# A list schedule with other durations and margins, and one copy moved from ScalarE to GpSimd

## The chip, the core and the metric

The kernel runs on one core of a Trainium2 chip. The metric is the device time of one execution in microseconds (us): the median of several runs. The profiler's engine names are used throughout: PE is TensorE's matmuls and PEld its weight loads, DVE is VectorE, ACT is ScalarE, POOL is GpSimd, and SPq is the queue of SyncE, from which this kernel issues all of its transfers. Each engine works through its own queue in order.

## The reference, cut to what matters

Two transformer blocks over 256 tokens of width 2048, in float32. The first block mixes sparse attention (NSA, 8 heads of 128) and an RWKV7 recurrence (16 heads of 64); the second has a layer A (differential attention) and a layer B (gated linear attention). Most of the work are products of the 2048-wide activations with weight matrices. The change sits in the recurrence:

```python
def rwkv7_mixer(feat, mu, w0, w2, a0, a2, k_k, k_a, r_k, ln_w, ln_b):
    ...
    aa = -kk
    bb = kk * a4
    def step(state, inp):
        r_t, w_t, k_t, v_t, a_t, b_t = inp
        sa = jnp.einsum('bhij,bhj->bhi', state, a_t)
        state = (state * w_t[:, :, None, :] + sa[..., None] * b_t[:, :, None, :]
                 + v_t[..., None] * k_t[:, :, None, :])
        return state, jnp.einsum('bhij,bhj->bhi', state, r_t)
    xs = tuple(z.transpose(1, 0, 2, 3) for z in (r4, w4, k4, v4, aa, bb))
    _, y = lax.scan(step, state0, xs)
```

The kernel doesn't step through 256 tokens. It takes them in 4 chunks of 64, and inside a chunk it solves a triangular system, for which a unit lower triangular matrix is inverted, in diagonal blocks of 32 by 32.

## The kernel before

**The weight stream.** Every weight matrix is cut into column groups (rk0, v0, kvc, rk2, v2, v3, q1, ...) and row tiles of 128. A `load` puts a raw tile `wr` into one of 4 buffers (512 KB a transfer, on SP's queue). ACT rounds it into the high part `wh` (fp32r), DVE subtracts to get the low part `wl`, 3 buffers each; then PE does three products per 128 columns (`wh` with `xh`, `wh` with `xl`, `wl` with `xh`) into `acc`. A tile of 128x1024 feeds 24 matmuls of 256 columns.

**The recurrence.** `rwkv_group(g, ...)` handles 4 of the 16 heads and is called for g = 0 to 3. Per group: decays `P`, the norm factor `ni` (a power on POOL), its square `sq` for the norm matmul `pnb`; small POOL copies `PC`; the four score matrices `AB` (matmuls `pA`); gathering of their diagonal blocks through DRAM (`db`, 4 transfers, then `blocks<-db`) so that 32 blocks of 32x32 lie on 32 partitions of the tile `blocks` (half `Y`); and the inversion by 30 steps of two POOL TENSOR_TENSORs each (`bt<-blocks`, `blocks<-blocks,bt`), a chain of 60 instructions, each depending on the one before. Then a transposed copy of `Y` into the other half `X`. `Y` and `X` go to DRAM (`dy`, `dx`), come back as `M1` (4 transfers; the trace calls them M) and `X` (2 transfers), and are used by the matmuls `pT` (on X), `pY`, `pX` and `pU`, after which the group's states follow chunk by chunk.

**Beside it** stand the compression products of NSA: `w1_00` to `w1_13` (weights, 8 loads of 512 KB, w_10 and so on in the rows) against windows, matmuls `ph`, then ACT's copy `hs`, matmuls `pz`, a tanh by ACT `ht`.

**What sets the order.** No order is written out by hand. Every call is recorded in a `Plan`; `flush` (L272, the line that all profile rows show) issues them in the order that `schedule` finds. It is a list schedule: it keeps a modelled time for each engine, lets each engine take the ready operation of the best priority, and appends it to the order. `Op.model` gives an operation's modelled duration, `LATENCY` what passes between two engines, `MARGIN` an addition for whatever TensorE waits for, `POOL_MARGIN` one for POOL's results that another engine waits for, `DMA_ISSUE` and its neighbours a transfer. Since the queues run in order, a modelled time that is too short puts an instruction ahead of work that could have gone first. The inversion chain is recorded with `nc.priority(1)`.

## Time and profile before

| what | before |
|---|---|
| median of 3 runs | 1500.48 us (1498.72 to 1500.61) |
| the profiled execution | 1499.45 us |
| its span, first to last instruction | 1497.7 us |
| PE busy | 1465.4 us (98%) |
| PEld, DVE, ACT, POOL busy | 89%, 63%, 51%, 20% |
| mean granted TensorE clock | 0.992 |

The profiled execution takes 1.75 us more than its span. Busy time is the union of an engine's instructions; matmuls are pipelined, so a row's duration (0.28 us for 256 columns at full clock) is longer than the distance to the next one (0.12 us). The granted clock is 1.00 at 2.4 GHz and 0.50 at 1.2 GHz. In rows, `[5.85 <-ACT hs]` says that the engine stood idle for 5.85 us before the instruction and that ACT's `hs` ended the wait.

### The profile page before, as it was taken

How to read it: one execution, taken by the hardware profiler on the slowest of the kernel's cores; microseconds unless marked ns; L12 is line 12 of the kernel's file. 1: busy time of each engine (PE TensorE's matmuls, PEld its weight loads, DVE VectorE, ACT ScalarE, POOL GpSimd, SP SyncE). 2: the span in 40 equal slices, each digit the busy share in tenths (PEclk: the TensorE clock that was granted, in tenths of full speed). 3: DMA queues.
4: the chain of work that ended last, by engine and by line, in shares of the span. 5: the costliest groups of instructions: out<-in, count | busy, mean ns of one | idle time of the engine just before them, and what ended most of it. 6: DMA issues, size and time to landing. Idle time of an engine off the chain costs nothing.

```text
span 1497.7 us, 25998 instructions
## 1 busy us (share of the span) xinstructions
PE 1465.4 (98%) x10205; PEld 1326.1 (89%) x10205; DVE 944.1 (63%) x1630; ACT 769.4 (51%) x1257; POOL 296.4 (20%) x398
## 2 busy tenths in 40 slices
PE   8999899999999999999999999999999999999999
PEld 8988789889989988778888888889999998988999
DVE  5775565375756765766666666756665459665554
ACT  6542354354454544757575757655443355455432
POOL 0139833812900000030404040100010001000000
PEclk9999999999999999999999999999999999999999
DMA  9546524444434467665555556555665554555563
GB/s 338 186 125 204 155 79 126 148 139 147 155 98 132 151 209 231 201 207 181 174 178 172 180 170 229 169 185 196 207 201 182 172 175 146 174 211 185 181 211 127
DMA packets 91963, 263.52 MB, mean 176 GB/s; under 512 B 19960, under 2 KB 26512, under 8 KB 91840
## 3 DMA queue, kind: packets, MB, share of 16 engines
q1 hardware_dynamic: 91840, 261.86, 54.5%
q8 instruction: 80, 1.31, 0.3%
q14 instruction: 43, 0.35, 0.1%
HBM read 253.92 MB, written 7.90 MB: 175 GB/s over the span
## 4 chain that ended last, share of the span: by engine, by line
PE 78%; POOL 3%; DVE 2%; DMA 1%; issue 1%; ACT 1%; SPq 0%; ACTq 0%; DVEq 0%; POOLq 0%
PE acc_Bo L272 6%; PE acc_Ao L272 6%; PE acc_o L272 6%; PE acc_Ag L272 6%; PE acc_Av L272 6%; PE acc_Aq L272 6%; PE acc_Bg L272 6%; PE acc_Ak L272 5%; PE acc_Bv L272 5%; PE acc_Bq L272 3%; PE acc_Bk L272 3%; PE acc_q L272 3%; PE acc_zb L272 3%; PE acc_za L272 2%; POOL bt L272 2%; POOL blocks L272 1%
## 5 line engine op out<-in xcount | busy, mean ns | idle before, releaser
L272 POOL TENSOR_TENSOR blocks<-blocks,bt 32x30 f32<-32x30 f32 (+14 forms) x120 | 84.3, 702 | 9.4
L272 POOL TENSOR_TENSOR bt<-blocks 32x30 f32<-32x30 f32 (+14 forms) x120 | 77.9, 649 | 9.2
L272 PE MATMUL acc_rk<-xh,wh_rk 128*128 128x256 f32 x256 | 74.1, 291 | 1.1 <-ACT wh_rk L272 0.9
L272 PE MATMUL acc_rk<-xh,wl_rk 128*128 128x256 f32 x256 | 73.8, 289 | 0.5 <-DVE wl_rk L272 0.5
L272 PE MATMUL acc_rk<-xl,wh_rk 128*128 128x256 f32 x256 | 73.1, 286 | 0.2 <-DVE xl L272 0.2
L272 PE MATMUL acc_Ao<-mAh,wl_Ao 128*128 128x256 f32 x256 | 72.7, 284 | 0.0
L272 PE MATMUL acc_Bo<-mBh,wl_Bo 128*128 128x256 f32 x256 | 72.6, 284 | 0.0
L272 PE MATMUL acc_Ao<-mAh,wh_Ao 128*128 128x256 f32 x256 | 72.5, 283 | 0.0
L272 PE MATMUL acc_Ao<-mAl,wh_Ao 128*128 128x256 f32 x256 | 72.4, 283 | 0.0
L272 PE MATMUL acc_Bo<-mBl,wh_Bo 128*128 128x256 f32 x256 | 72.4, 283 | 0.0
L272 PE MATMUL acc_Bo<-mBh,wh_Bo 128*128 128x256 f32 x256 | 72.3, 283 | 0.0
L272 DVE TENSOR_TENSOR wl_Bo<-wr_Bo,wh_Bo 128x1024 fp32r<-128x1024 f32 x32 | 39.2, 1225 | 45.0 <-ACT wh_Bo L272 45.0
L272 DVE TENSOR_TENSOR wl_rk<-wr_rk,wh_rk 128x1024 fp32r<-128x1024 f32 (+1 forms) x33 | 41.2, 1250 | 39.9 <-ACT wh_rk L272 36.7
L272 DVE TENSOR_TENSOR wl_Ao<-wr_Ao,wh_Ao 128x1024 fp32r<-128x1024 f32 x32 | 41.2, 1292 | 36.3 <-ACT wh_Ao L272 36.3
L272 DVE TENSOR_TENSOR wl_o<-wr_o,wh_o 128x1024 fp32r<-128x1024 f32 x32 | 39.2, 1225 | 37.2 <-ACT wh_o L272 37.2
L272 ACT ACTIVATE wh_Bo<-wr_Bo 128x1024 fp32r<-128x1024 f32 x32 | 33.9, 1058 | 53.1 <-PE acc_Bo L272 49.8
L272 DVE TENSOR_TENSOR wl_Bg<-wr_Bg,wh_Bg 128x1024 fp32r<-128x1024 f32 x32 | 39.2, 1224 | 34.8 <-ACT wh_Bg L272 34.8
L272 ACT ACTIVATE wh_rk<-wr_rk 128x1024 fp32r<-128x1024 f32 (+1 forms) x33 | 34.1, 1033 | 45.6 <-PE acc_rk L272 22.9
L272 DVE TENSOR_TENSOR wl_Bv<-wr_Bv,wh_Bv 128x824 fp32r<-128x824 f32 (+1 forms) x40 | 40.5, 1017 | 26.6 <-ACT wh_Bv L272 26.3
L272 ACT ACTIVATE wh_Ao<-wr_Ao 128x1024 fp32r<-128x1024 f32 x32 | 33.8, 1057 | 45.5 <-PE acc_Ao L272 38.7
L272 PE MATMUL acc_Bv<-wl_Bv,xBh 128*128 128x412 f32 (+1 forms) x160 | 56.4, 353 | 0.8 <-DVE wl_Bv L272 0.8
L272 DVE TENSOR_TENSOR wl_Ag<-wr_Ag,wh_Ag 128x1024 fp32r<-128x1024 f32 x32 | 39.2, 1224 | 28.0 <-ACT wh_Ag L272 28.0
(769 smaller groups left out, 5429.5 us busy)
## 6 DMA issues: line engine op xcount, KB each, us to landing
wr_o<-w SPq DMA_DIRECT2D x32, 512.0 KB, 4.0
wr_Aq<-w SPq DMA_DIRECT2D x32, 512.0 KB, 3.8
wr_Ak<-w SPq DMA_DIRECT2D x32, 512.0 KB, 3.5
wr_Av<-w SPq DMA_DIRECT2D x32, 512.0 KB, 4.3
wr_Ag<-w SPq DMA_DIRECT2D x32, 512.0 KB, 3.5
wr_Ao<-w SPq DMA_DIRECT2D x32, 512.0 KB, 3.5
wr_Bg<-w SPq DMA_DIRECT2D x32, 512.0 KB, 3.3
wr_Bo<-w SPq DMA_DIRECT2D x32, 512.0 KB, 4.2
```

The lines of the kernel that those rows point to most:

```text
L272: op.issued = getattr(getattr(self.nc, op.eng), op.method)(*op.args, **op.kw)
```

## The change

Three things change. `Op.model` gets other durations for TensorE (a matmul's cost no longer depends on its column position, and each matmul is given its `part`: the size and the position of the piece of the array that it uses) and for POOL's 32-partition TENSOR_TENSORs (200 + 2.9 ns an element where 150 + 1.65 or 2.1 stood). The planner's margins grow (`MARGIN` 200 to 700 ns, `POOL_MARGIN` 500 to 1500 ns), an issued transfer takes 340 ns of SP's modelled time instead of 60, a change of part size costs PE 170 ns, and a matmul at another column position than its predecessor counts half. And the transposed copy of the inverted blocks goes from ACT to POOL. No other operation is added or removed; all others may move in their queues.

```diff
@@ -110,15 +110,19 @@
         if self.dma:
             return n * out.shape[0] / 90
         if self.eng == "tensor":
-            at = out.start_partition() // 32
             if self.method == "transpose":
+                self.part = (4, 4, 0, 0)
                 return 109 if out.shape[-1] > 64 else 53
             cols, m = size(self.args[2]), size(self.args[1])
+            quarters = lambda n: 1 if n <= 32 else 2 if n <= 64 else 4
+            k = self.args[1].shape[0]
+            self.part = (quarters(k), quarters(m), self.args[1].start_partition() // 32 if k <= 64 else 0, out.start_partition() // 32 if m <= 64 else 0)
             if self.args[1].dtype == F32R:
-                return max(107, cols / 2.4)
+                return max(110, 13 + cols / 2.4)
             if m > 64:
-                return max(218, 4 + cols / 0.6)
-            return 3 + cols / 0.6 if at == 0 else 26.5 * -(-m // 32)
+                return max(220, 6 + cols / 0.6)
+            return 6 + cols / 0.6
         src = [x for x, write in self.uses if not write]
         psum = any(x.space == bass.MemoryType.PSUM for x in src)
         column = lambda x: isinstance(x, bass.AP) and size(x) == 1
@@ -138,8 +142,7 @@
         if self.kw.get("op") == OP.pow:
             return 300 + 165 * n
         if self.method == "tensor_tensor":
-            spread = all(any(not s for s, _ in x.ap[1:]) for x in src)
-            return 150 + (1.65 if spread else 2.1) * n
+            return 200 + 2.9 * n if out.shape[0] == 32 else 150 + 2.1 * n
         return 127 + 3.4 * n
 
 
@@ -157,9 +160,10 @@
         "gpsimd": {"tensor": 310, "vector": 60, "scalar": 180, "gpsimd": 102, "sync": 200},
     }
 
-    MARGIN, DMA_MARGIN, POOL_MARGIN = 200, (400, 1500), 500
+    MARGIN, DMA_MARGIN, POOL_MARGIN = 700, (400, 1500), 1500
     TABLE = 1283
-    DMA_ISSUE, DMA_START, DMA_EACH, DMA_END = 60, 950, 450, 990
+    SWITCH = 170
+    DMA_ISSUE, DMA_START, DMA_EACH, DMA_END = 340, 950, 450, 990
 
     def __init__(self, nc):
         self.nc = nc
@@ -169,6 +173,7 @@
         self.prio, self.chain, self.after = 0, None, ()
         self.free = dict.fromkeys(self.ENGINES, 0.0)
         self.log_table = False
+        self.part = None
         self.dma_queue = self.dma_engine = 0.0
         self.buffers, self.alive = {}, set()
         for eng in self.ENGINES:
@@ -382,7 +387,15 @@
             if eng == "scalar" and op.args[2] in (AF.Exp, AF.Tanh, AF.Ln) and self.log_table != (op.args[2] == AF.Ln):
                 self.log_table = not self.log_table
                 at += self.TABLE
-            op.start, op.end = at, at + op.cost
+            cost = op.cost
+            if eng == "tensor":
+                old, self.part = self.part, op.part
+                if old and old[:2] != op.part[:2]:
+                    at += self.SWITCH
+                elif old and old[3] != op.part[3]:
+                    cost /= 2
+            op.start, op.end = at, at + cost
             self.free[eng] = op.end
             op.seen = op.end + 200
 
@@ -882,7 +895,7 @@
                 tmp = self.sb(f"bt{g}_{k}", [128, 256], "bt", bufs=2)[gp, 0:k * n].rearrange("p (i j) -> p i j", j=n)
                 G.tensor_tensor(tmp, Y[:, 0:k, k:k + 1].to_broadcast([32, k, n]), Y[:, k:k + 1, k + 1:32].to_broadcast([32, k, n]), op=OP.mult)
                 G.tensor_tensor(Y[:, 0:k, k + 1:32], Y[:, 0:k, k + 1:32], tmp, op=OP.add)
-        S.activation(X.rearrange("p i j -> p j i"), Y, AF.Copy)
+        G.tensor_copy(X.rearrange("p i j -> p j i"), Y)
         dy = self.dram.tile([4, 4, 2, 32, 32], F32, name=f"dy{g}")
         nc.sync.dma_start(dy.rearrange("q h c s t -> (q h c) s t"), Y)
         dx = self.dram.tile([4, 4, 2, 32, 32], F32, name=f"dx{g}")
```

ACT's queue around the copy of group 0. Before, the copy stands between two `wh` of the rk2 weights and ahead of `hs`:

```order
L272 ACTIVATE wh_rk_10_470<-wr_rk_10_469 128x1024
L272 ACTIVATE wh_rk_12_474<-wr_rk_12_473 128x1024
L272 ACTIVATE blocks<-blocks 32x32x32
L272 ACTIVATE wh_rk_14_478<-wr_rk_14_477 128x1024
L272 ACTIVATE hs_458<-ph_443 128x128
L272 ACTIVATE ht_462<-hz_461 128x30
L272 ACTIVATE wh_v_0_495<-wr_v_0_494 128x1024
```

ACT's queue at the same place after:

```order
L277 ACTIVATE wh_rk_10_470<-wr_rk_10_469 128x1024
L277 ACTIVATE wh_rk_12_474<-wr_rk_12_473 128x1024
L277 ACTIVATE hs_458<-ph_443 128x128
L277 ACTIVATE ht_462<-hz_461 128x30
L277 ACTIVATE wh_rk_14_478<-wr_rk_14_477 128x1024
L277 ACTIVATE kc<-pkc 128x2x15
L277 ACTIVATE wh_v_0_495<-wr_v_0_494 128x1024
```

The copy is gone from ACT, and `hs` and `ht` stand ahead of the last `wh` of rk2. No copy of `blocks` is left in ACT's queue for any of the four groups.

SP's queue at the same place, before: the group's inverse goes out with dy and dx, and comes back as M and X. `w_10` to `w_13` are weights for the `ph` matmuls.

```order
L272 DMA wr_v_4_497<-w 128x1024
L272 DMA w_10_468<-cw 128x1024
L272 DMA dy_230<-blocks 32x1024
L272 DMA wr_v_8_500<-w 128x1024
L272 DMA dx_231<-blocks 32x1024
L272 DMA cw_481<-cw 128x128
L272 DMA w_11_472<-cw 128x1024
L272 DMA w_12_476<-cw 128x1024
L272 DMA wr_v_12_503<-w 128x1024
L272 DMA M_240<-dy_230 32x8x32 x4
L272 DMA w_13_480<-cw 128x1024
L272 DMA X_241<-dx_231 32x8x32 x2
```

SP's queue at the same place after:

```order
L277 DMA wr_v_0_494<-w 128x1024
L277 DMA dy_230<-blocks 32x1024
L277 DMA w_10_468<-cw 128x1024
L277 DMA wr_v_4_497<-w 128x1024
L277 DMA M_240<-dy_230 32x8x32 x3
L277 DMA dx_231<-blocks 32x1024
L277 DMA M_240<-dy_230 32x8x32
L277 DMA w_11_472<-cw 128x1024
L277 DMA w_12_476<-cw 128x1024
L277 DMA cw_481<-cw 128x128
L277 DMA wr_v_8_500<-w 128x1024
L277 DMA X_241<-dx_231 32x8x32 x2
```

dy stands ahead of `w_10` and of `wr_v_4` where it stood behind both. The load that starts group 0's inversion (blocks<-db_199) stands behind `wr_kvc_415` (the third load of kvc), where it stood behind `wr_kvc_427` (the seventh).

POOL's queue where group 0's inversion starts, before: `PC` and `ni` belong to the next group (1).

```order
L272 MEMSET p02p 128x2
L272 MEMSET M_240 32x8x32 x2
L272 MEMSET p12p 128x2
L272 COPY PC_326<-P_314 64x2 x6
L272 TENSOR_TENSOR ni_320<-n_319,mhalf 128x8
L272 MEMSET blocks 32x32
L272 TENSOR_TENSOR bt_30_200<-blocks 32x30
L272 TENSOR_TENSOR blocks<-blocks,bt_30_200 32x30
L272 TENSOR_TENSOR bt_29_201<-blocks 32x58
```

POOL's queue after, the start of the inversion and a piece further on:

```order
L277 MEMSET p02p 128x2
L277 MEMSET blocks 32x32
L277 TENSOR_TENSOR bt_30_200<-blocks 32x30
L277 TENSOR_TENSOR blocks<-blocks,bt_30_200 32x30
L277 TENSOR_TENSOR bt_29_201<-blocks 32x58
...
L277 COPY PC_326<-P_314 64x2
L277 TENSOR_TENSOR bt_22_208<-blocks 32x198
L277 COPY PC_326<-P_314 64x2
L277 TENSOR_TENSOR blocks<-blocks,bt_22_208 32x22x9
L277 TENSOR_TENSOR ni_320<-n_319,mhalf 128x8
L277 TENSOR_TENSOR bt_21_209<-blocks 32x210
```

The inversion stands ahead of group 1's `PC` copies and `ni`, which are now spread between its steps. POOL's copy of `blocks` stands behind the last step of its own group and the first step of the next. On PE, 1182 matmuls stood ahead of the first `pT` of group 0, and 1115 do now (of those gone, 58 are 256-column products of the weight stream and 9 are `ph`); ahead of the first `ph` of `w_10` stand 25 products of the weight stream fewer.

## Rows read from the trace of the kernel before

**Rows 1.** The page: busy time, share of the span and instructions of each engine
```profile
PE 1465.4 (98%) x10205; PEld 1326.1 (89%) x10205; DVE 944.1 (63%) x1630; ACT 769.4 (51%) x1257; POOL 296.4 (20%) x398
```
**Rows 2.** Stretches: PE, PEld, DVE, ACT, POOL busy (instructions); PEclk; DMA share; GB/s
```profile
105.00:112.00 7.00, 4.39 (x21) 3.35 (x20) 3.46 (x6) 1.06 (x1) 6.17 (x16) 0.76 0.45 156
...
149.00:160.00 11.00, 5.15 (x42) 4.84 (x40) 2.17 (x5) 4.41 (x6) 8.52 (x23) 0.69 0.58 178
...
295.00:307.00 12.00, 6.00 (x32) 5.51 (x32) 5.67 (x11) 4.89 (x5) 2.75 (x10) 0.72 0.50 132
...
416.00:426.00 10.00, 7.16 (x36) 6.49 (x35) 6.57 (x16) 4.92 (x14) 0.00 (x0) 0.66 0.66 185
```
**Rows 3.** Stretches, PE alone: length, PE busy, PEclk, DMA share, GB/s; their sum
```profile
155.69:159.40 3.71, 3.71 (x18) 0.50 0.96 329
...
sum 17.98, PE 16.49; mean PE 4.12
```
**Rows 4.** Timeline at 149 to 156 us, PE and then ACT: start, duration, instruction, [idle before]
```profile
149.44 0.28 PE L272 MATMUL acc_rk<-xh,wh_rk 128*128 128x256 f32 x1
149.56 0.28 PE L272 MATMUL acc_rk<-xl,wh_rk 128*128 128x256 f32 x1
155.69 0.64 PE L272 MATMUL pz<-cst,hs 128*128 128x32 f32 x2 [5.85 <-ACT hs L272]
...
152.71 1.93 ACT L272 ACTIVATE blocks<-blocks 32x1024 f32<-32x1024 f32 x1 [7.96 <-POOL blocks L272]
...
155.39 0.24 ACT L272 ACTIVATE hs<-ph 128x128 f32<-128x128 f32 x1
```
**Rows 5.** Timeline at 298 us, ACT
```profile
298.30 1.93 ACT L272 ACTIVATE blocks<-blocks 32x1024 f32<-32x1024 f32 x1 [10.13 <-POOL blocks L272]
```
**Rows 6.** Timeline at 413 to 419 us, ACT and then SP's queue
```profile
413.45 2.08 ACT L272 ACTIVATE blocks<-blocks 32x1024 f32<-32x1024 f32 x1 [5.75 <-POOL blocks L272]
...
418.95 0.35 SPq L272 DMA_DIRECT2D wr_q<-w  x1
```
**Rows 7.** Timeline at 100 to 111 us, POOL and then DVE
```profile
100.67 5.78 POOL L272 COPY PC<-P 64x2 f32<-64x2 f32 x6 [1.97 <-ACT P L272]
...
109.77 1.19 POOL L272 TENSOR_TENSOR bt<-blocks 32x84 f32<-32x84 f32 x1
...
108.21 0.50 DVE L272 TENSOR_SCALAR sq<-ni 128x512 f32<-128x512 f32 x1 [2.92 <-POOL ni L272]
...
109.45 1.32 DVE L272 TENSOR_TENSOR wl_kvc<-wr_kvc,wh_kvc 128x1024 fp32r<-128x1024 f32 x1
```
**Rows 8.** The waits by pair: us in total, times, longest
```profile
ACT blocks L272 <- POOL blocks L272: 23.8, 3, 10.1
```
**Rows 9.** The tile blocks: duration ns min/median/max, first and last start, forms
```profile
L272 POOL TENSOR_TENSOR bt<-blocks x120: 225/560/1677, 108.2 to 412.9; 32x30 f32<-32x30 f32 x8, 32x58 f32<-32x58 f32 x8, 32x84 f32<-32x84 f32 x8, 32x108 f32<-32x108 f32 x8
...
L272 ACT ACTIVATE blocks<-blocks x4: 1927/2004/2116, 152.7 to 413.5; 32x1024 f32<-32x1024 f32 x4
```
**Rows 10.** GpSimd's copies: the tile PC, and the timeline at 1250 us
```profile
L272 POOL COPY PC<-P x24: 178/284/4661, 66.8 to 330.4; 64x2 f32<-64x2 f32 x24
...
1250.82 3.82 POOL L272 COPY k<-kd 128x128 f32<-128x128 f32 x1 [135.78 <-DVE kd L272]
```
**Rows 11.** Timeline, SP's queue and then PE; DMA landing of the tile dx
```profile
98.06 0.31 SPq L272 DMA_DIRECT2D blocks<-db  x1
...
152.70 0.34 SPq L272 DMA_DIRECT2D dy<-blocks  x1
...
160.67 0.92 SPq L272 DMA_DIRECT2D X<-dx  x2
...
159.57 0.64 PE L272 MATMUL ph<-w,win 128*32 128x128 f32 x16
...
169.62 0.56 PE L272 MATMUL pT<-X,AB 32*32 32x32 f32 x23
...
DMA to landing us min/median/max: 2.0/3.0/5.8
```

## Prediction

> **What bounds the kernel now.** The page's busy times come first: PE is busy for 1465.4 of the 1497.7 us of the span [rows 1]. So PE is the bound, and a change of order can win only two things: the 32.3 us in which PE stands idle, and time in which its clock is low. The next view is the table of stretches, which shows where these are. Four short places hold most of it [rows 2]: idle there is 7.00 − 4.39 = 2.61, 11.00 − 5.15 = 5.85, 12.00 − 6.00 = 6.00 and 10.00 − 7.16 = 2.84 us, together 17.30. The other 15.0 us lie scattered over some 1460 us. In the same four stretches, and in no other of the table, the granted clock is well under 1. Looked at closely, each idle piece is followed by matmuls at a clock of 0.50, that is 1.2 GHz; the four pieces hold 16.49 us of PE work [rows 3]. What that costs: in the piece shown 18 instructions take 3.71 us; at the 0.12 us between two 256-column products at full clock [rows 4] they would take 2.16, so 42% are lost, or 6.9 us over the four; if all of them took exactly twice as long it would be 8.25. I take 7.
>
> Then the timelines say who is late at each place. At 149.56 us PE stops for 5.85 us until ACT's `hs`. ACT had not been busy: it stood idle for 7.96 us in front of its copy of `blocks`, which waits for the last step of GpSimd's inversion at 152.7 us, and `hs`, at 155.39, was queued behind it [rows 4]. At 298.30 it is the same with `wh_v`: ACT waits 10.13 us for the inversion, with the weights' rounding behind the copy [rows 5]. At 413.45 ACT waits 5.75 us and, after its 2.08 us copy, has a heap of softmax work and two `wh_q` to catch up on; besides, a load of `wr_q` is issued only at 418.95 [rows 6], since `dy`, `dx` and the M transfers ahead of it in SP's queue waited for the same inversion. Summed by pair, ACT's waits for the inversion are 23.8 us in three pieces [rows 8]: three of four groups. The fourth place, the stretch from 105 us, is another thing: PE waits for `pnb`, that for DVE's `sq`, which starts at 108.21 after 2.92 us of idling, since POOL needed 5.78 us for six copies of 64x2 and then made `ni` [rows 7].
>
> **The change, part by part.**
>
> *The copy leaves ACT.* Nothing of ACT's queue waits for the inversion any more. At places 2 and 3 ACT then has its `hs` and `wh_v` done when their inputs are there, some 5.85 and 6.00 us earlier than PE needed to stop for. At place 4 the copy's wait and its 2.08 us go too. Gain: the idle time of these places, 14.7 us.
>
> *The new durations of POOL's steps.* Group 0's inversion takes 152.70 − 108.2 = 44.5 us [rows 9, 11]. The old order, with ACT's copy too early at three groups, shows that it was planned as shorter. Now its `blocks` load stands four weight loads earlier in SP's queue, and one such load feeds 24 products of 0.12 us, so 2.88 us of PE: issue at 98.06 − 11.5 = 86.5 us [rows 11].
>
> *`ni` and `PC` of group 1* now stand between steps of group 0's inversion, `ni` after 18 of 60. They no longer keep `sq` waiting if the norm is at hand; the six copies are not in front of `ni` in a block, since only two are. Gain at place 1: 2.61 us, perhaps 2.
>
> *The clock* returns with the idle time: 7 us of the sum, 6.9 to 8.25 by the above.
>
> So far −17.3 − 7 = −24.3.
>
> *POOL's copy, 4 times.* The trace has no such copy on POOL. From below: ACT's took 1.93 to 2.12 us [rows 9]. From nearby: POOL's steps have a median of 0.56 us [rows 9] at a mean of 165 elements (30, 58, 84 and so on, 4960 over 30 steps), 3.4 ns an element, which gives 3.5 us for 1024; they read two operands and the copy one. From far: `k<-kd` took 3.82 us for 128 elements a partition at a time when DVE was busy without a gap [rows 10], which would give 8 x 3.82 = 30.6 us. I take 2.5 us, by the steps, which run on the same partitions and at the same hour. Cover: `X` is needed only by `dx`, and ahead of `dx` in SP's queue stand the `dy` transfer and three M transfers that wait for it. The next group's inversion is behind the copy on POOL and 2.5 us later for it, in a chain of 45 to 50; its cover is counted in the next term. On the path: 0.
>
> *A new wait: the inverse comes back late.* On PE the first `pT` stands 58 products and 9 `ph` earlier, 58 x 0.12 + 9 x 0.04 = 7.3 us. It ran at 169.62 [rows 11]; less the lost time of places 1 and 2 (2.61 + 5.85 idle, and 42% of two low-clock pieces of 4.12 us, their mean [rows 3], 3.5; together 12.0), less 7.3, PE is there at 150.3 us. The inverse: `blocks` issued at 86.5, landed after 3.0 (2.0 to 5.8, by the transfers of `dx` [rows 11]), 44.5 us of steps, and between them `ni` (108.2 − 106.45 = 1.7) and six `PC` (6 x 0.284 at their median [rows 10], 5.78 as at 100.67 [rows 7]): it ends at 89.5 + 44.5 + 3.4 to 7.5 = 137.4 to 141.5 us. From the end of the steps to the issue of the last X transfer it took 160.67 + 0.92 − 152.70 = 8.9 us, with about as many transfers between, and 3.0 to land: X is there at 149.3 to 153.4, with slow landings at 159. So PE waits for 0 to 3.1 us, at the outside 8. `w_10` now stands behind `dy` on SP: issued within 1 us of the inversion's end and landed 3 later, at 141.4 to 145.5; its `ph` ran at 159.57, less 12.0, less 25 x 0.12, so it is wanted at 144.6. That fits by medians and no more. Behind `dy` stand `w_10`, `wr_v_4` and everything after, but of raw weight tiles there are four. I take +2 (0 to +8, the clock's fall included) for groups 0 and 1 together.
>
> *Order on the array.* In PE's order 355 neighbouring pairs of small matmuls of one part size now lie at different positions, where 273 did; changes of size are 175 instead of 176. 23 alternating `pT` pass in 0.56 us, 16 `ph` at one position in 0.64 [rows 11], 0.024 against 0.040 each: 82 x 0.016 = 1.3. I take −1 (0 to −1.3).
>
> *The wider margin for PE's operands* can only touch the 15.0 us elsewhere: −1 (from −4 to +3; the places are many and each is tiny).
>
> Sum: −24.3 + 2 − 1 − 1 = −24.3. The profiled execution took 1499.45 us, which gives 1475.2; it lies 1.0 below the median of the runs, so on that scale 1476.
>
> **A rule that speaks against it.** In the trace, POOL's step of 84 elements at 109.77 took 1.19 us and ended at 110.96, just after DVE's `wl` subtract from 109.45 to 110.77 [rows 7]; and the first of the six copies that took 5.78 us began while DVE ran without a gap [rows 7], where the median copy takes 0.284 [rows 10]. The Trainium skill ("SBUF — State Buffer", "Who interferes with whom") says that a DVE instruction with two inputs in SBUF and a GpSimd instruction that reads SBUF shut each other out, for as long as the first of the two runs. By that rule the copy can start late by one subtract or several, and the trace agrees with it in the 1.19 us step. The same section would have the next `wl` subtract wait for the end of the copy, which no row here shows; at 2.5 us, with three `wl` buffers of 2.88 us of PE work each, it would stay hidden.
>
> **The rivals.**
>
> (a) *The inverse is late at groups 0 and 1.* Both have no slack to speak of. For it: `w_10` and X fit to within 2 us by medians, and landings go up to 5.8. Against: four raw tiles and the margin. Price: the outer case of 8 us once, some 2 to 4 at group 1: about 9 more than forecast, 1485.
>
> (b) *The change doesn't do what it says: the wait goes from ACT to SP's queue.* `dy` stands as early as before or earlier, and the loads behind it are held until the inversion ends. For it: place 4 has it already, with `wr_q` at 418.95 [rows 6]. Against: at 149 and 298 us PE waited for ACT and not for a raw tile. Price: place 4 loses 2.84 us of idling [rows 2] and 42% of a low-clock piece of 4.12 [rows 3], 4.6 us; kept there and new at two more, 13.7 us: 1490. Were SP's waits to cost at each place what ACT's do now, only place 1's 2.61 us would be won: 1498, no change that can be told.
>
> (c) *Slower: POOL's copy is starved by DVE.* A copy that runs as `k<-kd` did takes 30.6 us [rows 10]. At groups 0 and 1 nearly all of the excess of 28 us goes to PE's wait for X: 1476 + 2 x 28 = 1532. It decides from the point where a copy takes 2.5 + (24 + 3) / 2 = 16 us. The rule of the Trainium skill above would allow it, where DVE's two-input work is dense. Against it: steps of the inversion ran all the time beside such work with a median of 0.56 us and at most 1.677 [rows 9].
>
> **How the numbers follow.** Chances: the forecast 0.64, (a) 0.17, (b) 0.13, (c) 0.06. What a measurement of this kernel can tell from no change is 0.2%, 3 us. Faster by more: 0.64 + 0.17 and 0.09 of (b), 0.90; within it 0.04, (b) at its full price; slower 0.06. The range: the forecast's own goes from −17.3 − 8.25 − 4 − 1.3 = −30.9 (1469) to −17.3 − 6.9 + 3 + 8 = −13.2 (1487). To leave out no more than 2 in 10 it reaches over (a) to the edge of (b): 1468 to 1490.
>
> **What would show it.** In the profile after: no copy of `blocks` on ACT and no wait of ACT for POOL's `blocks`; four POOL copies of 2 to 3.5 us; PE busy at about 1457 (1465.4 less 7 and 1) and idle at 15 to 18 us; in the stretches 105, 149, 298 and 416, clock 1.00. (a) would show as a wait of PE for the transfer of X or of `w` at about 140 to 155 us with clock 0.50 behind it; (b) as waits of ACT for `wr` transfers while SP stands at `dy`; (c) as a POOL copy of over 15 us. The forecast is wrong if PE's idle time stays above 25 us, or if its busy time doesn't fall.

## The result, and the profile after

The changed kernel takes 1491.28 us (median of 5 runs, 1488.82 to 1492.53); the kernel before took 1500.61 beside it (1498.72 to 1501.98). The ratio is 0.9938, 95% interval 0.9925 to 0.9951. It is faster, but by 9.3 us and not by 24, and the time lies 1.3 us above the forecast's range of 1468 to 1490. The profiled execution took 1491.25 us, its span is 1489.4, that is 8.3 less than before.

The page's busy times of the changed kernel, to be held against [rows 1]:

```profile
PE 1462.6 (98%) x10205; PEld 1322.8 (89%) x10205; DVE 952.9 (64%) x1630; ACT 762.0 (51%) x1253; POOL 313.3 (21%) x402
```

PE is busy for 2.8 us less and idle for 26.8 us where it was 32.3. The forecast had 8 less and some 16, and named idle time above 25 us as a sign of being wrong. DVE is busy for 8.8 us more, with as many instructions.

The most useful cut is between the two blocks, at the first transpose of the second block (`tp`). The stretches of the kernel before:

```profile
0.00:614.10 614.10, 589.69 (x4901) 0.98 0.52 165
614.10:1497.70 883.60, 875.75 (x5304) 1.00 0.57 184
```

And of the changed kernel (length, PE busy, PEclk, DMA share, GB/s):

```profile
0.00:597.10 597.10, 582.42 (x4901) 0.99 0.53 169
597.10:1489.40 892.30, 880.17 (x5304) 0.99 0.57 182
```

The first block, with the four places, is 17.0 us shorter: 9.7 us less of idling (24.4 to 14.7) and 7.3 us less of PE time. The second block, of which the forecast said only that the wider margins might touch it, is 8.7 us longer: 12.1 us of idling instead of 7.9, and 4.4 us more of PE time for the same 5304 products.

**What went as forecast.** ACT has no copy of `blocks` and no wait for GpSimd's `blocks`; the waits of 5.85, 6.00 and 2.84 us at places 2 to 4 [rows 2] are not there. GpSimd's copies, in the rows of the tile:

```profile
L277 POOL COPY blocks<-blocks x4: 2048/2114/2132, 145.2 to 396.4; 32x1024 f32<-32x1024 f32 x4
```

2.1 us each, where 2.5 were taken. The inverse of group 0 was done early, and PE still had to wait for it, as the term of the new wait said. The timeline, SP's queue and then PE:

```profile
144.85 0.34 SPq L277 DMA_DIRECT2D dy<-blocks  x1
...
152.42 1.16 SPq L277 DMA_DIRECT2D X<-dx  x2
...
154.80 0.64 PE L277 MATMUL ph<-w,win 128*32 128x128 f32 x16 [1.43 <-DMA w<-cw]
158.18 0.87 PE L277 MATMUL pT<-X,AB 32*32 32x32 f32 x32 [1.59 <-DMA X<-dx]
```

`dy` left 7.9 us earlier than in [rows 11], the first `pT` came 11.4 us earlier, and on the way there PE waited 1.43 us for a `w` and 1.59 for X, 3.0 in all (forecast: 2).

**Place 1 stayed.** The same wait for `sq` as in [rows 7], timeline of POOL, DVE and PE:

```profile
104.95 1.69 POOL L277 TENSOR_TENSOR ni<-n,mhalf 128x8 f32<-128x8 f32 x1
...
106.98 1.07 DVE L277 SCALAR_TENSOR_TENSOR k<-fr,par,k 128x256 f32<-128x256 f32 x2
107.98 1.61 DVE L277 TENSOR_TENSOR wl_kvc<-wr_kvc,wh_kvc 128x1024 fp32r<-128x1024 f32 x1
109.51 0.41 DVE L277 TENSOR_SCALAR sq<-ni 128x512 f32<-128x512 f32 x1
...
109.98 1.11 PE L277 MATMUL pnb<-cst,sq 128*128 128x128 f32 x4 [2.79 <-DVE sq L277]
```

`ni` ends at 106.64, 1.5 us earlier than before. But DVE, which had stood idle for it before, is now late itself: `sq` stands behind two `k` and a `wl` of 1.61 us (1.22 for the `wl` at 105.06 us). All this runs beside GpSimd's inversion, which started behind 108 us before and starts at 90.8 us now.

**The moved copy cost something at group 1.** DVE, ACT and PE when GpSimd's copy runs (194.25 to 196.36 us):

```profile
194.59 2.53 DVE L277 COPY AV<-fv 128x256 f32<-128x256 f32 x2
...
198.81 0.72 ACT L277 ACTIVATE P<-L 128x256 f32<-128x256 f32 x2 [1.83 <-DVE L L277]
199.44 0.49 ACT L277 ACTIVATE sq<-fk,par 128x256 f32<-128x256 f32 x1
...
199.98 0.83 PE L277 MATMUL pn<-cst,sq 128*128 128x2 f32 x6 [1.15 <-ACT sq L277]
```

The first of the two DVE copies lasted 2.13 us and ended 0.36 us after GpSimd's copy did; the tile's row has it as the longest of eight, and in the kernel before none took more than 0.29:

```profile
L277 DVE COPY AV<-fv x8: 284/386/2134, 53.6 to 307.5; 128x256 f32<-128x256 f32 x8
```

From it hang `L`, ACT's `P` and `sq` behind it, and PE's `pn`: 1.15 us of idling and then, from 201.75 us on, a granted clock of 0.50 for 16 products.

**The second block.** POOL and PE in layer B, timeline:

```profile
1235.91 3.55 POOL L277 COPY k<-kd 128x128 f32<-128x128 f32 x1 [136.49 <-DVE kd L277]
...
1239.52 0.80 PE L277 MATMUL pB<-q,k 128*128 128x128 f32 x2 [2.94 <-POOL k L277]
```

And PE's stretch behind the wait:

```profile
1239.52:1246.00 6.48, 6.48 (x37) 0.50 0.11 44
```

This copy took 3.82 us before [rows 10], hardly different. What differs is PE's queue: before, 7 products of `acc_Bv` stood between the `pB` part that needs `kd` and the one that needs `k`, and the wait was 1.49 us:

```profile
1254.69 0.49 PE L272 MATMUL pB<-q,k 128*128 128x128 f32 x2 [1.49 <-POOL k L272]
```

Now none stands there, the wait is 2.94 us, and 6.5 us at 1.2 GHz follow. Nearby are further waits of 0.91 and 0.80 us. The timeline has one more at 943 us (1.16 us, for DVE's `mAl`), and at the start of the block three short waits, 1.6 us together, are followed by another piece at the lower clock (PE's stretch):

```profile
601.00:604.40 3.40, 3.40 (x12) 0.50 0.07 7
```

At half the clock these two pieces, 9.9 us, cost some 5 us (an estimate); the second block's PE time grew by 4.4.

### The profile page after: what moved, and what is told of

Its sections match the earlier page's. It is cut to its first block, busy times and chain, and to the rows that moved or that the text cites. A ratio compares the mean times of both kernels' runs of the same rounds, so it can differ in the third digit from the quotient of the medians.

```text
span 1489.4 us, 25986 instructions
## 1 busy us (share of the span) xinstructions
PE 1462.6 (98%) x10205; PEld 1322.8 (89%) x10205; DVE 952.9 (64%) x1630; ACT 762.0 (51%) x1253; POOL 313.3 (21%) x402
## 4 chain that ended last, share of the span: by engine, by line
PE 90%; DVE 6%; ACT 1%; DMA 1%; issue 1%; POOL 1%; SPq 0%; DVEq 0%; ACTq 0%
PE acc_Bo L277 6%; PE acc_Ao L277 6%; PE acc_Aq L277 6%; PE acc_o L277 6%; PE acc_Ak L277 6%; PE acc_Av L277 6%; PE acc_rk L277 6%; PE acc_Bg L277 6%; PE acc_Ag L277 5%; PE acc_Bv L277 5%; PE acc_Bq L277 3%; PE acc_Bk L277 3%; PE acc_zb L277 3%; PE acc_q L277 3%; PE acc_v L277 3%; PE acc_za L277 2%
## 5 line engine op out<-in xcount | busy, mean ns | idle before, releaser
L277 POOL TENSOR_TENSOR bt<-blocks 32x30 f32<-32x30 f32 (+14 forms) x120 | 83.0, 692 | 9.0
L277 PE MATMUL acc_Bv<-wh_Bv,xBl 128*128 128x412 f32 (+1 forms) x160 | 57.1, 357 | 0.0
```

The lines of the kernel that those rows point to most:

```text
L277: op.issued = getattr(getattr(self.nc, op.eng), op.method)(*op.args, **op.kw)
```

## The experiments

All of them change the plan's numbers or one engine, and leave the computation as it is. "Base" is the fourth, from which most others start. First block and second block are lengths in the profile, cut as above; ratios are to the kernel before on the same chip. A profile is of one execution, which can lie some us from the median: run 1's took 1506.7 us, run 10's 1487.9 and run 4's 1476.6.

| run | median us | ratio (95%) | first | second |
|---|---|---|---|---|
| before | 1500.6 | | 614.1 | 883.6 |
| changed | 1491.3 | 0.9938 (0.9925 to 0.9951) | 597.1 | 892.3 |
| 1 copy only | 1501.6 | 1.0006 (0.9992 to 1.0020) | 619.0 | 885.9 |
| 2 numbers only | 1497.4 | 0.9977 (0.9968 to 0.9986) | 606.5 | 890.9 |
| 3 second block as before | 1485.3 | 0.9892 (0.9877 to 0.9908) | 600.7 | 883.5 |
| 4 base: copy and GpSimd's cost | 1478.7 | 0.9851 (0.9833 to 0.9868) | 591.9 | 882.9 |
| 5 base, wide margins | 1479.1 | 0.9852 (0.9839 to 0.9865) | 587.8 | 889.6 |
| 6 base, TensorE's numbers | 1501.5 | 1.0006 (0.9995 to 1.0016) | 606.5 | 892.8 |
| 7 base, issue time | 1483.8 | 0.9891 (0.9869 to 0.9912) | 596.4 | 882.5 |
| 8 changed, k on DVE | 1490.0 | 0.9918 (0.9904 to 0.9932) | 602.6 | 887.2 |
| 9 base, pace | 1495.2 | 0.9967 (0.9954 to 0.9980) | 604.9 | 888.6 |
| 10 base, part switch | 1486.2 | 0.9907 (0.9891 to 0.9922) | 597.3 | 888.8 |
| 11 changed, old pace | 1481.1 | 0.9877 (0.9863 to 0.9891) | 588.2 | 890.0 |
| 12 margins in first block | 1473.2 | 0.9826 (0.9812 to 0.9840) | 587.9 | 883.6 |
| 13 true numbers, big margins | 1485.6 | 0.9897 (0.9878 to 0.9916) | 593.8 | 888.3 |
| 14 run 12, k on DVE | 1472.6 | 0.9814 (0.9793 to 0.9836) | 587.7 | 882.9 |

**1. The copy alone**, in the kernel before:

```diff
-        S.activation(X.rearrange("p i j -> p j i"), Y, AF.Copy)
+        G.tensor_copy(X.rearrange("p i j -> p j i"), Y)
```

> The kernel before with the transposed copy on GpSimd and none of the new numbers. Its order in the second block is that of the kernel before, row for row, so whatever it gains is gained in the first block. Theory (the wait sat in ACT's queue, so taking the copy off ACT is what removes it): the idle times at places 2 to 4 (14.7 us) and their clock go, but PE then reaches the first pT some 12 us earlier and waits there 5 to 8 us for X: 1488 to 1493. Rival (the planned durations are what matters, and with the old ones the wait only moves to PE's wait for X or to SP's queue): 1496 to 1501.

The rival was right: 1501.6 us, no gain. ACT's waits are gone and come back on PE and on SP's queue. PE's timeline in this run:

```profile
161.79 1.08 PE L272 MATMUL ph<-w,win 128*32 128x128 f32 x16 [6.10 <-DMA w<-cw]
...
309.74 1.24 PE L272 MATMUL pT<-X,AB 32*32 32x32 f32 x32 [3.92 <-DMA X<-dx]
```

And SP's line in the table of waits (us in total, times, longest):

```profile
SPq L272 <- POOL blocks L272: 31.8, 4, 13.5
```

SP's queue stands at `dy` for 31.8 us in all, and PE waits 6.10 us for the `w` queued behind it. Taking the copy off ACT moves the wait; the planned length of the inversion has to change with it.

**2. The numbers alone**: the changed kernel with the copy back on ACT.

```diff
-        G.tensor_copy(X.rearrange("p i j -> p j i"), Y)
+        S.activation(X.rearrange("p i j -> p j i"), Y, AF.Copy)
```

> The changed kernel with the transposed copy back on ACT. Theory (the copy is half of the gain): with true durations ACT's copy is planned later, its waits shrink from 23.8 us to under 10, but it still takes 2 us of ACT each time and the order around it is tighter: first block 3 to 8 us behind the changed kernel, second block as in the changed kernel: 1494 to 1499. Rival (the numbers alone do it): 1490 to 1493, as the changed kernel.

As the theory had it: 1497.4 us. Neither half alone brings what both bring.

**3. The second block planned with the numbers of before**, the first block's order unchanged row for row:

```diff
                 nc.flush(tc)
+            Op.OLD, nc.MARGIN, nc.POOL_MARGIN, nc.DMA_ISSUE = True, 200, 500, 60
             with tc.tile_pool(name="work2", bufs=1, reuse_waits="tile") as work:
```

(`Op.OLD` selects the durations of before in `Op.model`.)

> The changed kernel with the numbers of before from the second block on; the first block's order is that of the changed kernel, row for row. In the changed kernel PE enters the second block 17.0 us earlier than before and ends 8.3 us earlier. Theory (the second block's new order, planned with the new numbers, loses those 8.7 us): 1481 to 1485. Rival (the loss is handed over by the first block, as late weights or a low clock, whatever the order): 1489 to 1493.

1485.3 us, at the upper end of what the theory said, and the second block takes 883.5 us as before: the 8.7 us are lost by its own new order and by nothing that it is handed. Run 2, with the changed kernel's order there, has 890.9. By the medians run 3 is 5.9 us faster than the changed kernel; its profiled execution had a first block 3.6 us longer (see the last section).

**4. The base: the copy, and GpSimd's cost alone** of all the numbers, in the kernel before:

```diff
-            spread = all(any(not s for s, _ in x.ap[1:]) for x in src)
-            return 150 + (1.65 if spread else 2.1) * n
+            return 200 + 2.9 * n if out.shape[0] == 32 else 150 + 2.1 * n
...
-        S.activation(X.rearrange("p i j -> p j i"), Y, AF.Copy)
+        G.tensor_copy(X.rearrange("p i j -> p j i"), Y)
```

> The kernel before with the copy on GpSimd and, of all new numbers, only the cost of GpSimd's 32-partition steps (200 + 2.9 ns an element). Second block as before. Theory (these two carry the first block's gain; the margins, the transfer and TensorE numbers add little there): 1482 to 1486. Rival (margins and issue time are needed to keep PE from waiting for X and the weights): 1488 to 1494.

1478.7 us, 3.3 below the theory's range: two of the change's edits alone are 12.6 us faster than the whole change. Its stretches:

```profile
0.00:591.90 591.90, 580.88 (x4901) 1.00 0.53 171
591.90:1474.80 882.90, 875.68 (x5304) 1.00 0.57 184
```

Four rows of its timeline (PE, SP, DVE, PE):

```profile
108.22 0.93 PE L271 MATMUL pnb<-cst,sq 128*128 128x128 f32 x4 [2.60 <-DVE sq L271]
...
160.15 0.34 SPq L271 DMA_DIRECT2D dy<-blocks  x1
...
160.93 2.90 DVE L271 TENSOR_TENSOR wl_v<-wr_v,wh_v 128x1024 fp32r<-128x1024 f32 x1
...
178.69 0.69 PE L271 MATMUL pT<-X,AB 32*32 32x32 f32 x32
```

Place 1's wait, 2.60 us, is still in the base. Group 0's inverse is done 15 us later than in the changed kernel (160.15 against 144.85), and still PE doesn't wait for it: the first `pT` stands behind 1131 products of the weight stream, not behind 968, and runs at 178.69. So at this place what counts is how far the consumer stands behind in PE's queue, not how early the inverse is. The question then was which of the other numbers takes these 163 products (at 0.12 us, 19.6 us) away.

**5. Base and the wide margins:**

```diff
-    MARGIN, DMA_MARGIN, POOL_MARGIN = 200, (400, 1500), 500
+    MARGIN, DMA_MARGIN, POOL_MARGIN = 700, (400, 1500), 1500
```

> The kernel of the experiment with the copy and GpSimd's cost (1478.7 us) plus the two wider margins (700 and 1500 ns). It asks which of the new numbers costs the 12.6 us by which the changed kernel is slower than that. Theory (the wider margins do: whatever PE waits for is planned later, so its consumers stand together in clumps, in the second block above all): second block 5 to 8 us longer, 1484 to 1489. Rival (TensorE's durations do it): no change, 1476 to 1481.

Half a miss. The time didn't change (1479.1), so the margins are not where the 12.6 us go. But the second block is 6.7 us longer, as the theory had it, and the first 4.1 shorter: place 1's wait is gone there.

**6. Base and TensorE's numbers** (durations, part switch, halved cost), the change's own lines:

```diff
-                return max(107, cols / 2.4)
+                return max(110, 13 + cols / 2.4)
...
+                if old and old[:2] != op.part[:2]:
+                    at += self.SWITCH
+                elif old and old[3] != op.part[3]:
+                    cost /= 2
```

> The same base plus TensorE's new durations, the part switch and the halved cost at another position; margins and issue time as before. Rival to the margins (these durations reorder PE's small matmuls and shift the second block): 1484 to 1490. Theory (the margins are to blame): 1476 to 1481. If both families cost, both lie at 1481 to 1486.

The rival to the margins, and more of it than expected: 1501.5 us; all of the base's gain is gone. PE's wait at place 1, 2.60 us in the base, is 5.18, and there is one for X, which the base has not:

```profile
108.05 1.12 PE L277 MATMUL pnb<-cst,sq 128*128 128x128 f32 x4 [5.18 <-DVE sq L277]
...
161.06 0.88 PE L277 MATMUL pT<-X,AB 32*32 32x32 f32 x32 [2.84 <-DMA X<-dx]
```

960 products stand ahead of that `pT`. A further wait, 2.99 us for `sq` at 211.65 us, is not in the base either.

**7. Base and the issue time:**

```diff
-    DMA_ISSUE, DMA_START, DMA_EACH, DMA_END = 60, 950, 450, 990
+    DMA_ISSUE, DMA_START, DMA_EACH, DMA_END = 340, 950, 450, 990
```

> The same base plus the issue time of 340 ns alone. The second block's order is that of the base, row for row, so only the first block can move. If the late weights and the late X at group 0 in the changed kernel (3.0 us of PE's idle time and the low clock behind it) come from the loads' new places in SP's queue, 1481 to 1485; otherwise 1476 to 1481.

1483.8 us, with a wide spread (1480.69 to 1492.34), a loss of some 5 us, all in the first block. The time is as expected for late weights and a late X at group 0, but this profile shows no such wait; what it lost there is open.

**8. The changed kernel with layer B's `k` on DVE:**

```diff
-            G.tensor_copy(k2[:, :, 1], d[:, :, 1])
+            V.tensor_copy(k2[:, :, 1], d[:, :, 1])
```

> The changed kernel with layer B's four copies of k moved from GpSimd to DVE; the first block's order is that of the changed kernel, row for row. In the changed kernel PE waits 2.94 us for the first of these copies, which takes GpSimd 3.55 us while DVE runs two-input instructions without a gap, and 6.8 us at 1.2 GHz follow. Theory (that wait is most of the second block's loss): 5 to 6 us faster than the changed kernel, 1485 to 1487. Rival (the loss is spread over the second block's order, or DVE's next instructions are held up as much): 1489 to 1492.

Inconclusive in time (1490.0, in the rival's range; the intervals of the two ratios overlap). In the profile the second block is 5.1 us shorter and the wait at `pB` falls from 2.94 to 0.50 us, with no low clock behind it, as the theory had it, but the first block of that execution, with the changed kernel's order row for row, took 602.6 us instead of 597.1. The clock accounts for most of that: in this execution it was 0.50 for 3.3 us from 12.9 us on, behind a wait of 1.68 us (1.66, and no fall, in the changed kernel's), and for 10.1 us from 159.7 us on.

**9. Base and the pace alone:**

```diff
-                return max(107, cols / 2.4)
+                return max(110, 13 + cols / 2.4)
             if m > 64:
-                return max(218, 4 + cols / 0.6)
-            return 3 + cols / 0.6 if at == 0 else 26.5 * -(-m // 32)
+                return max(220, 6 + cols / 0.6)
+            return 6 + cols / 0.6 if at == 0 else 26.5 * -(-m // 32)
```

> The base (copy on GpSimd, GpSimd's cost; 1478.7 us) plus TensorE's longer durations alone (110 or 13 + cols/2.4 instead of 107, and so on), without the part switch and the halved cost. The traced distance of two 256-column products is 0.12 us, so the old 107 ns has PE run some 11% too fast in the plan, and whatever another engine makes stands that much further back in PE's queue: slack that the true pace takes away. Theory (the slack is what carries): ahead of group 0's first pT stand 998 products here, 1131 in the base; PE waits for X, pnb and the weights again: 1490 to 1499. Rival (the switch and the halved cost, which reorder the small matmuls, lose the time): 1477 to 1482.

1495.2 us, in the theory's range. Thirteen nanoseconds per product (107 to 119.7), and they are the true ones, cost 16.5 us. Of the 13 us in the first block 4.5 are idle time (604.90 − 589.33 against 591.90 − 580.88):

```profile
0.00:604.90 604.90, 589.33 (x4901) 0.99 0.53 167
604.90:1493.50 888.60, 877.91 (x5304) 1.00 0.58 183
```

Place 1's wait is as in the base; new is the same wait one group later:

```profile
106.67 0.66 PE L271 MATMUL pnb<-cst,sq 128*128 128x128 f32 x4 [2.45 <-DVE sq L271]
...
207.35 0.66 PE L271 MATMUL pnb<-cst,sq 128*128 128x128 f32 x4 [2.43 <-DVE sq L271]
```

Further ones, for DVE's `hz` (1.24 us at 151 us) and `e` (up to 1.08, at 382 to 404), are shorter. For X and the weights, which the theory named too, PE doesn't wait at group 0. The other 8.5 us count as busy: the clock is 0.50 in three pieces of 3.3 us where the base has one, and the rest would be short waits that no idle time shows, since a row's 0.28 us covers more than the 0.12 us to the next one; that is argued and not shown.

**10. Base and the part switch alone**, with the old pace:

```diff
-            return 3 + cols / 0.6 if at == 0 else 26.5 * -(-m // 32)
+            return 3 + cols / 0.6
...
+                if old and old[:2] != op.part[:2]:
+                    at += self.SWITCH
+                elif old and old[3] != op.part[3]:
+                    cost /= 2
```

> The base plus the part switch (170 ns) and the halved cost at another position alone, with the old pace. 1044 products stand ahead of group 0's first pT, 87 fewer than in the base, since small matmuls that stand together are planned shorter than before. Theory (slack): less is lost than with the pace, 1482 to 1490, and in the first block, since the second one's order is the base's but for a few rows. Rival (these two lose all of it): 1495 to 1502.

1486.2 us, within the theory's range: 7.5 us above the base by the medians, 11.3 between the two profiled executions. Of these 5.4 are in the first block and 5.9 in the second, where the order is the base's but for a few rows from the first `pB` on. The second block's loss is not the switch's own. GpSimd's copy of `k`, 3.82 us in the base, took 4.42 here, and PE's wait for it was 2.27 us instead of 1.48 (timeline of POOL and PE, then PE's stretch behind the wait):

```profile
1234.89 4.42 POOL L277 COPY k<-kd 128x128 f32<-128x128 f32 x1 [135.78 <-DVE kd L277]
...
1239.36 0.80 PE L277 MATMUL pB<-q,k 128*128 128x128 f32 x2 [2.27 <-POOL k L277]
...
1239.36:1245.80 6.44, 6.44 (x28) 0.50 0.23 66
```

That wait, the low clock behind it (an estimate of 3.2 us: 6.4 at half) and two waits of 0.79 and 0.76 us at 635 us, where the order is still the base's, make nearly all of the 5.9.

**11. The changed kernel with the old pace:**

```diff
-                return max(110, 13 + cols / 2.4)
+                return max(107, cols / 2.4)
             if m > 64:
-                return max(220, 6 + cols / 0.6)
-            return 6 + cols / 0.6
+                return max(218, 4 + cols / 0.6)
+            return 3 + cols / 0.6
```

> The changed kernel with TensorE's old pace (107, 218, 3 + cols/0.6) and everything else of the change. Theory (slack): 64 more products ahead of group 0's first pT than in the changed kernel, so the waits for w and X there go (3.0 us and the clock): 1481 to 1487. Rival (with margins of 700 and 1500 ns the pace no longer matters): 1489 to 1493.

1481.1 us, at the lower end of the theory's range: the whole change, less the pace, gains twice as much as the whole change. The theory's mechanism came out only in part. 1032 products stand ahead of the first `pT`, and PE still waits there, with a low clock behind it, as it waits 0.77 us for a `w` at 141 us (timeline, then PE's stretch):

```profile
163.33 0.88 PE L277 MATMUL pT<-X,AB 32*32 32x32 f32 x32 [1.67 <-DMA X<-dx]
...
164.40:167.80 3.40, 3.40 (x36) 0.50 0.15 25
```

What went are the waits at place 1 (2.79 to 0.31 us) and at 199 us (1.15 to none). Nor does the number of products ahead of that `pT` rank the runs: with 1032 the first block takes 588.2 us, with 1044 (run 10) 597.3, and with 1131 (run 4) 591.9.

**12. Base, wide margins in the first block alone** (run 5's line, and):

```diff
                 nc.flush(tc)
+            nc.MARGIN, nc.POOL_MARGIN = 200, 500
             with tc.tile_pool(name="work2", bufs=1, reuse_waits="tile") as work:
```

> The base plus the wide margins in the first block only; the second block is planned with the margins of before. With the margins throughout, the first block took 3.9 us less than in the base and the second 6.7 us more. Theory (the two blocks can be added): 1470 to 1474. Rival (the order of the second block pays for the earlier start): 1477 to 1480.

1473.2 us: the two blocks can be added. It beats the kernel before by 1.7% and the changed one by 1.2%. Its stretches:

```profile
0.00:587.90 587.90, 580.79 (x4901) 1.00 0.55 172
587.90:1471.50 883.60, 875.98 (x5304) 1.00 0.58 184
```

**13. True numbers with large margins in the first block** (run 3 with other margins):

```diff
-    MARGIN, DMA_MARGIN, POOL_MARGIN = 700, (400, 1500), 1500
+    MARGIN, DMA_MARGIN, POOL_MARGIN = 3000, (400, 1500), 5000
```

> The changed kernel's true numbers (pace, part, issue, GpSimd's cost) in the first block with margins of 3000 and 5000 ns instead of 700 and 1500; the second block is planned with the numbers of before, as in the experiment that gave 1485.3. Ahead of group 0's first pT stand 1069 products (968 there, 1131 in the base), ahead of the second group's pnb 755 (703). Theory (what the first block lacks is slack, whichever number provides it): PE's waits at 107, 154 and 199 us go, 1472 to 1480. Rival (the true pace makes a worse order however late the consumers stand): 1483 to 1488.

The time is the rival's, 1485.6; the profile says more. The waits at 107 and 199 us are gone and that at the first `pT` is down to 0.29 us (others of 1.4 to 2.6 us stand elsewhere, two of them for `w`), and the weight stream of the first block ends at 591.4 us, 9 us earlier than in run 3. But at the end of the block, where nothing is left to put between, PE waits twice for the second block's input:

```profile
593.79 1.19 PE L288 MATMUL tp<-cst,y 128*128 128x128 f32 x4 [2.40 <-DVE y L288]
598.33 1.25 PE L288 MATMUL tp<-cst,y 128*128 128x128 f32 x4 [3.35 <-DVE xAl L288]
```

and a low clock follows; that uses up what was won. One margin for all waits is not the slack of the old pace.

**14. Run 12 with layer B's `k` on DVE** (the edit of run 8):

> The fastest so far (copy on GpSimd, its cost, wide margins in the first block only; 1473.2 us) with layer B's four copies of k on DVE. The one idle piece of PE left in the second block that is longer than 1 us is the 1.48 us wait for the first of them. Theory: that goes, 1471 to 1473. Rival (DVE's own work is later by the copies, 0.2 to 0.3 us each, and PE waits for it instead): 1473 to 1475.

1472.6 us, the fastest of all. The 1.48 us wait is gone in the profile; in time the two cannot be told apart.

## Why the prediction was wrong, step by step

- **What bounds the kernel, the four places, their causes**: right for places 2 to 4. Their 14.7 us of idling went; place 1's stayed and new waits came, so that the first block's idle time fell by 9.7 us in all. With the PE time the block gained 17.0 us.
- **"Nothing of ACT's queue waits for the inversion any more. ... Gain: 14.7 us"**: right only together with the longer planned inversion. Run 1 has the one without the other, and gains nothing; rival (b) of the forecast, the wait moving to SP's queue, is just what it shows (31.8 us).
- **"Gain at place 1: 2.61 us, perhaps 2"**: failed. `ni` comes earlier, DVE is late instead. The step looked at `ni` and not at what stands ahead of `sq` on DVE while GpSimd's inversion runs beside it.
- **"POOL's copy ... On the path: 0"**: nearly. The price of 2.5 us was right (2.1). The forecast did consider that the next `wl` would be held and called that hidden by the three `wl` buffers; what was held at group 1 was a copy with no such buffer behind it, ahead of `L`, `P` and `sq`: DVE for 2.13 us, PE for 1.15 and a fall of the clock. Rival (c) expected DVE to starve GpSimd; it was GpSimd that held DVE.
- **"A new wait: +2 (0 to +8)"**: right in its size, 3.0 us of idling at group 0, for w and for X, but with luck. The load was issued at 86.6 us, as worked out (86.5); the inversion then took from 90.8 to 144.85 us, 54 us, and ended 3.4 to 7.5 us later than the forecast's 137.4 to 141.5. PE, held at place 1, came to `pT` at 156.6 instead of 150.3, and the two errors nearly cancel. In the executions of runs 3 and 8, with the same order, a low clock follows these waits as well.
- **The clock, 7 us**: about right in the first block (7.3 us less of PE time), but place 1's fall stays and new waits bring new falls: at 201.75 us, 3.4 us at the passage between the blocks, and 6.5 us in layer B.
- **"The wider margin for PE's operands can only touch the 15.0 us elsewhere: −1 (from −4 to +3; the places are many and each is tiny)"**: this is the step that failed. The new numbers made a new order of the whole program, and the second block lost 8.7 us by it, where the term allowed for +3 at the most; run 3 shows it. That (8.7 us), place 1 (2.6 not gained) and the copy at group 1 (1.15), with the low clock behind the last two, make most of the 15 us between the forecast of 1476 and the measurement. Of that block's loss the margins alone make 6.7 us (run 5), TensorE's pace alone 5.7 (run 9); they don't add up.
- **What the forecast had no term for at all**: the pace. It took the durations of TensorE to be a matter of the array's order ("−1"). Run 4, which has neither these numbers nor the margins, comes within 3 us of the forecast; what the forecast put at −1 and −1 on top of it stands for +12.6. The reading of the runs is this: the old 107 ns, where the trace has 120, had PE run too fast in the plan; whatever comes from another engine was put behind more products than it needed, and from chain to chain this adds up: with the true pace 455 products stand ahead of group 0's first `pA` and 998 ahead of its first `pT`, with the old one 529 and 1131 (run 9 against run 4, counted in PE's queue). That the pace costs the time, runs 4, 9 and 11 show from both sides: true pace added, −16.5 us of the gain; true pace taken out of the change, +10.2 (by the ratios 17 and 9). That it does so as slack is argued: the waits for X and `w` that it should have removed in run 11 are still there, 1.67 and 0.77 us. The margins that the change widened in its place give only a part of the time back.

What stays open: what run 9's second block loses its 5.7 us by. It is not the place at `pB`: the waits there are 0.94 and 1.14 us where the base has one of 1.48, and no low clock follows; three waits of 0.75 us for `zAq` are new. That slack as such is what the first block lacks is supported by the stream's end in run 13, but its total, the rival's, did not follow: another order made by the true pace, and not less slack, is not ruled out.

## What to carry to other kernels

In a list schedule for engines that run in order, an error in a modelled duration can act as a safety margin; here a truer pace cost time, and that reading fits most of the runs. Before a model is made truer, ask which waits its error covers; correct first the duration that is too short for the producer (here GpSimd's steps, worth some 22 us with the copy), and the consumer's pace only together with a margin that replaces it, tested part by part and block by block. And when a planner's numbers change, the forecast must cover every stage that it orders, not only the one that the numbers were made for.

## What the runs showed of the hardware

- GpSimd's transposed copy held DVE. `AV<-fv`, a copy with one input, took 2.13 us beside it in the changed kernel where the kernel before has 0.28, and a `wl` subtract 2.90 instead of 1.22 in run 4. The Trainium skill ("SBUF — State Buffer", "Who interferes with whom") says that the two engines share a pair of ports, that a DVE instruction with two inputs in SBUF contends for it with a GpSimd instruction that reads SBUF, a copy only in a mode that uses both ports, and that whoever issues first blocks the other for the whole instruction. The `wl` row agrees, in the direction that the forecast had found no row for; in which mode the `AV` copy ran, no row shows. DVE needed 8.8 us more for the same 1630 instructions; the copy alone (run 1, 947.6 us busy) and the numbers alone (run 2, 948.8) each have about half of that over the 944.1 before.
- The same waits in the same order were followed by a low clock in one execution and not in another. Run 3 and the changed kernel have one first block, row for row. In run 3 PE waited 1.64 and 1.78 us at 153 to 158 us, and the granted clock was then 0.50, that is 1.2 GHz:

```profile
159.60:166.00 6.40, 6.40 (x80) 0.50 0.11 44
```

In the changed kernel's execution the waits were 1.43 and 1.59 us, and it stayed at 2.4:

```profile
158.20:168.00 9.80, 9.80 (x177) 1.00 0.44 167
```

That accounts for most of the 3.6 us by which the first blocks of the two differ, and it sets a floor to what one profile of such a kernel can tell.
